# Multiply and GELU of two 1024 x 4096 arrays: all of x kept in SBUF, loads of 8192 down to 2048 columns, one store per 4096 columns

## The chip, the cores and the metric

The kernel runs on one core of one Trainium2 chip. The metric is device time of one execution in microseconds (us). Each profile is one execution; its span runs from the first instruction to the last, and the device time of the same execution is about 1.7 us longer. All runs quoted here were in the fast state, at clock 1.0.

## The reference

```python
def reference(x, y):            # two float32 arrays of 1024 x 4096
    z = x * y
    return (0.5 * z * (1 + np.tanh(np.sqrt(2 / np.pi) * (z + 0.044715 * z ** 3)))).astype(np.float32)
```

33.55 MB must be read and 16.78 MB written. Arithmetic is one multiply and one activation per element.

## The kernel before

Each array is seen as 128 partitions of 32768 columns. Seven tiles of 4096 columns and four of 1024 go through the same steps; x is overwritten by the product and by the result.

```python
def _process_tile(nc, sbuf, tile_f, x_r, y_r, out_r, c0, c1):
    ts_ = c1 - c0
    x_tile = sbuf.tile([128, tile_f], x_r.dtype)
    y_tile = sbuf.tile([128, tile_f], y_r.dtype)
    nc.sync.dma_start(out=x_tile[:, :ts_], in_=x_r[:, c0:c1])      # loads: SyncE queue
    nc.sync.dma_start(out=y_tile[:, :ts_], in_=y_r[:, c0:c1])
    nc.vector.tensor_mul(out=x_tile[:, :ts_], in0=x_tile[:, :ts_], in1=y_tile[:, :ts_])
    nc.scalar.activation(out=x_tile[:, :ts_], in_=x_tile[:, :ts_],
                         func=mybir.ActivationFunctionType.Gelu_apprx_tanh)
    nc.scalar.dma_start(out=out_r[:, c0:c1], in_=x_tile[:, :ts_])  # store: ScalarE queue
# ... (cut)
    big_tiles = [4096] * 7
    small_tiles = [1024] * 4
# ... (cut)
    big_sbuf = ctx.enter_context(tc.tile_pool(name="big", bufs=3))
    small_sbuf = ctx.enter_context(tc.tile_pool(name="small", bufs=8))
```

The stores are issued from the queue of the engine that does the activations.

## Time and profile before

| | before |
|---|---|
| device time, median of 4 runs | 123.83 us (123.77 to 123.91) |
| span of the profiled execution | 122.5 us |
| bytes moved, mean rate | 50.33 MB, 411 GB/s |
| VectorE / ScalarE busy | 35.8 / 30.7 us |

Read the DMA row of the page first: it is full in every slice but the first and the last, while both compute engines idle over two thirds of the time. A transfer-bound kernel like this one can lose time only where the transfer engines are empty or slow. The prediction below shows the lines.

### The profile page before, as it was taken

How to read it: one execution, taken by the hardware profiler on the slowest of the kernel's cores; microseconds unless marked ns; L12 is line 12 of the kernel's file. 1: busy time of each engine (PE TensorE's matmuls, PEld its weight loads, DVE VectorE, ACT ScalarE, POOL GpSimd, SP SyncE). 2: the span in 40 equal slices, each digit the busy share in tenths (PEclk: the TensorE clock that was granted, in tenths of full speed). 3: DMA queues.
4: the chain of work that ended last, by engine and by line, in shares of the span. 5: the costliest groups of instructions: out<-in, count | busy, mean ns of one | idle time of the engine just before them, and what ended most of it. 6: DMA issues, size and time to landing. Idle time of an engine off the chain costs nothing.

```text
span 122.5 us, 134 instructions
## 1 busy us (share of the span) xinstructions
DVE 35.8 (29%) x11; ACT 30.7 (25%) x12; POOL 0.2 (0%) x4
## 2 busy tenths in 40 slices
DVE  0000770590000580068000085019300039555000
ACT  4000029009100019001900004700650000884200
POOL 0000000000000000000000000000000000000000
DMA  4999999989999999999999999999999999999994
GB/s 112 428 433 428 439 439 433 369 337 439 439 433 428 433 428 428 428 433 428 428 433 439 439 433 433 428 428 433 433 428 428 428 417 407 411 413 455 397 423 164
DMA packets 4752, 50.33 MB, mean 411 GB/s; under 512 B 528, under 2 KB 528, under 8 KB 2064
## 3 DMA queue, kind: packets, MB, share of 16 engines
q1 hardware_dynamic: 3168, 33.56, 65.7%
q10 hardware_dynamic: 1584, 16.78, 32.2%
HBM read 33.55 MB, written 16.78 MB: 411 GB/s over the span
## 4 chain that ended last, share of the span: by engine, by line
DMA 76%; DVE 8%; ACT 7%; SPq 1%; issue 1%; DVEq 0%
DMA y_tile<-in_y_dram 30%; DMA out_dram<-x_tile 24%; DMA x_tile<-in_x_dram 22%; DVE x_tile L18 8%; ACT x_tile L20 7%; SPq L15 1%; SPq L16 0%; DVEq L18 0%
## 5 line engine op out<-in xcount | busy, mean ns | idle before, releaser
L18 DVE TENSOR_TENSOR x_tile<-x_tile,y_tile 128x4096 f32<-128x4096 f32 (+1 forms) x11 | 35.8, 3261 | 77.4 <-DMA y_tile<-in_y_dram 77.4
L20 ACT ACTIVATE x_tile<-x_tile 128x4096 f32<-128x4096 f32 (+1 forms) x11 | 29.4, 2684 | 82.8 <-DVE x_tile L18 82.4
L20 ACT ACT_TABLE_LOAD x1 | 1.3, 1283 | 0.7 <-PEq L87 0.7
L87 POOL MEMSET const-bfloat16-1.0<- 128x1 bf16 x1 | 0.1, 101 | 0.0
L87 POOL MEMSET const-uint8-127<- 128x1 uint8 x1 | 0.1, 101 | 0.0
L87 POOL MEMSET const-float32-0.0<- 128x1 f32 x1 | 0.1, 98 | 0.2 <-issue 0.2
L87 POOL MEMSET const-float32-1.0<- 128x1 f32 x1 | 0.1, 98 | 0.0
## 6 DMA issues: line engine op xcount, KB each, us to landing
x_tile<-in_x_dram SPq DMA_DIRECT2D x7, 2048.0 KB, 16.3
y_tile<-in_y_dram SPq DMA_DIRECT2D x7, 2048.0 KB, 20.7
out_dram<-x_tile ACTq DMA_DIRECT2D x7, 2048.0 KB, 13.8
x_tile<-in_x_dram SPq DMA_DIRECT2D x4, 512.0 KB, 21.2
y_tile<-in_y_dram SPq DMA_DIRECT2D x4, 512.0 KB, 20.5
out_dram<-x_tile ACTq DMA_DIRECT2D x4, 512.0 KB, 8.6
```

The source lines that it names most:

```text
L15: nc.sync.dma_start(out=x_tile[:, :ts_], in_=x_r[:, c0:c1])
L18: nc.vector.tensor_mul(out=x_tile[:, :ts_], in0=x_tile[:, :ts_], in1=y_tile[:, :ts_])
L20: nc.scalar.activation(out=x_tile[:, :ts_], in_=x_tile[:, :ts_], func=mybir.ActivationFunctionType.Gelu_apprx_tanh,)
L87: nc = _bacc.Bacc("TRN2", target_bir_lowering=False, num_devices=1)
```

## The change

The intent: no load should ever wait for a store to free its buffer. x gets a tile of its own for each load (128 KB per partition in all), y alternates between two buffers of 32 KB. Loads start at 8192 columns and shrink toward the end; compute and stores go in steps of 4096 columns (2048 for the last two loads).

```diff
+LOADS = [8192, 8192, 8192, 4096, 2048, 2048]
+STEP = 4096
 ...
-    big_sbuf = ctx.enter_context(tc.tile_pool(name="big", bufs=3))
-    small_sbuf = ctx.enter_context(tc.tile_pool(name="small", bufs=8))
 ... (the loop over tiles and _process_tile are removed)
+    x_pool = ctx.enter_context(tc.tile_pool(name="xs", bufs=1))
+    y_pool = ctx.enter_context(tc.tile_pool(name="ys", bufs=2))
+    a = 0
+    for i, w in enumerate(LOADS):
+        xt = x_pool.tile([P, w], F32, name=f"x{i}", tag=f"x{i}")
+        yt = y_pool.tile([P, max(LOADS)], F32, name=f"y{i}", tag="y")
+        nc.sync.dma_start(out=xt[:, :], in_=x_r[:, a : a + w])
+        nc.sync.dma_start(out=yt[:, :w], in_=y_r[:, a : a + w])
+        for c in range(0, w, STEP):
+            d = min(w, c + STEP)
+            nc.vector.tensor_mul(out=xt[:, c:d], in0=xt[:, c:d], in1=yt[:, c:d])
+            nc.scalar.activation(out=xt[:, c:d], in_=xt[:, c:d], func=GELU)
+            nc.scalar.dma_start(out=out_r[:, a + c : a + d], in_=xt[:, c:d])
+        a += w
```

Loads are called x0, y0 to x5, y5 below; the nine steps, their multiplies, activations and stores are numbered 0 to 8. Steps 0 to 6 have 4096 columns, steps 7 and 8 have 2048.

More of the change, by code (lines that the diff above doesn't have):

```diff
@@ L7 @@
 from concourse._compat import with_exitstack
-def _process_tile(nc, sbuf, tile_f, x_r, y_r, out_r, c0, c1):
-    ts_ = c1 - c0
-    x_tile = sbuf.tile([128, tile_f], x_r.dtype)
-    y_tile = sbuf.tile([128, tile_f], y_r.dtype)
-    nc.sync.dma_start(out=x_tile[:, :ts_], in_=x_r[:, c0:c1])
-    nc.sync.dma_start(out=y_tile[:, :ts_], in_=y_r[:, c0:c1])
-    nc.vector.tensor_mul(out=x_tile[:, :ts_], in0=x_tile[:, :ts_], in1=y_tile[:, :ts_])
-    nc.scalar.activation(
-        out=x_tile[:, :ts_],
-        in_=x_tile[:, :ts_],
-        func=mybir.ActivationFunctionType.Gelu_apprx_tanh,
-    )
-    nc.scalar.dma_start(out=out_r[:, c0:c1], in_=x_tile[:, :ts_])
+F32 = mybir.dt.float32
+GELU = mybir.ActivationFunctionType.Gelu_apprx_tanh
+LOADS = [8192, 8192, 8192, 4096, 2048, 2048]
+STEP = 4096
 @with_exitstack
@@ L42 @@
     out_r = out.flatten_outer_dims().rearrange("(p a) c -> p (a c)", p=P)
-    total_f = x_r.shape[1]
-    big_tiles = [4096] * 7
-    small_tiles = [1024] * 4
-    if sum(big_tiles) + sum(small_tiles) != total_f:
-        big_tiles = []
-        remaining = total_f
-        while remaining >= 4096 * 2:
-            big_tiles.append(4096)
-            remaining -= 4096
-        small_tiles = []
-        while remaining > 0:
-            ts_ = min(1024, remaining)
-            small_tiles.append(ts_)
-            remaining -= ts_
-    big_f = max(big_tiles) if big_tiles else 1024
-    small_f = max(small_tiles) if small_tiles else 1024
-    big_sbuf = ctx.enter_context(tc.tile_pool(name="big", bufs=3))
-    small_sbuf = ctx.enter_context(tc.tile_pool(name="small", bufs=8))
-    c0 = 0
-    for ts_ in big_tiles:
-        _process_tile(nc, big_sbuf, big_f, x_r, y_r, out_r, c0, c0 + ts_)
-        c0 += ts_
-    for ts_ in small_tiles:
-        _process_tile(nc, small_sbuf, small_f, x_r, y_r, out_r, c0, c0 + ts_)
-        c0 += ts_
+    assert sum(LOADS) == x_r.shape[1]
+    x_pool = ctx.enter_context(tc.tile_pool(name="xs", bufs=1))
[12 more added lines that the diff above has]
+        a += w
 _INS = ['x', 'y']
```

## The prediction

> **What bounds it now.** I read the page first (busy shares, GB/s by slice), then the chain that ended last, the groups by form, the windows, and last the trace's single DMA packet records.
>
> ```profile
> span 122.5 us, 134 instructions
> DVE 35.8 (29%) x11; ACT 30.7 (25%) x12; POOL 0.2 (0%) x4
> DMA  4999999989999999999999999999999999999994
> GB/s 112 428 433 428 439 439 433 369 337 439 439 433 428 433 428 428 428 433 428 428 433 439 439 433 433 428 428 433 433 428 428 428 417 407 411 413 455 397 423 164
> ...
> HBM read 33.55 MB, written 16.78 MB: 411 GB/s over the span
> ```
>
> The multiply engine and the activation engine are idle more than two thirds of the time; the transfers are busy in every slice but the first and last. 50.33 MB at the plateau of 431 GB/s is 116.8 us of the 122.5. So only three things can change the time: idle transfer engines at the start, in the middle, and at the end.
>
> ```profile
> 0.00:1.74 1.74, 0.00 (x0) 1.02 (x1) 0.20 (x4) 1.00 0.00 0
> ...
> 24.00:26.00 2.00, 2.00 (x1) 0.00 (x0) 0.00 (x0) 1.00 0.85 262
> 26.00:98.00 72.00, 19.01 (x5) 18.08 (x5) 0.00 (x0) 1.00 1.01 431
> 98.00:111.50 13.50, 8.01 (x4) 6.42 (x4) 0.00 (x0) 1.00 1.02 416
> 111.50:119.40 7.90, 1.22 (x1) 1.31 (x2) 0.00 (x0) 1.00 1.00 419
> ...
> 121.30:122.50 1.20, 0.00 (x0) 0.00 (x0) 0.00 (x0) 1.00 0.00 0
> ```
>
> (Columns: stretch, length, VectorE, ScalarE and GpSimd busy with counts, clock, DMA share, GB/s.) Lost now: 1.7 us before the first packet and about 1 us of slow first packets; (431-262) x 2 us = 0.34 MB, 0.8 us, when the first store begins; some 0.6 us to 1024-column transfers (416 and 419 over 21 us); 1.2 us of receipt and end. In the tail there is **no gap**: the last load's last packet ends at 111.4 us (packet records), and five stores of 4.19 MB in all are queued or about to be, which keep the engines busy to 121.3 us while the last tile is multiplied and activated:
>
> ```profile
> 111.95 1.22 DVE L18 TENSOR_TENSOR x_tile<-x_tile,y_tile 128x1024 f32<-128x1024 f32 x1 [1.29 <-DMA y_tile<-in_y_dram]
> 113.21 1.06 ACT L20 ACTIVATE x_tile<-x_tile 128x1024 f32<-128x1024 f32 x1 [1.46 <-DVE x_tile L18]
> 114.29 0.34 ACTq L26 DMA_DIRECT2D out_dram<-x_tile  x1
> ```
>
> **What the Trainium skill says.** "HBM Reference", Specifications, has a core streaming alone at about 425 GB/s; the trace agrees, 431. "SBUF — State Buffer", SBUF size, leaves about 208 KiB per partition; the change takes 128 KB of x and 64 KB of y, so it fits. "DMA: Bandwidth & Descriptors", Queues, rings and completion order, says that each engine takes a packet from one queue row, then from the next. The trace agrees, and shows what a packet is here: one partition's row of a transfer, 16384 B in 611 ns, or 4096 B in 159 ns. Where both queues hold 16384 B packets the load and store shares are near equal (in 2 us bins from 26.7 to 32.7 us the loads have 205, 152 and 225 GB/s, the stores 225, 279 and 206); where loads have 4096 B packets against stores of 16384 B, the bin at 98.7 to 100.7 us has 91 GB/s of loads and 339 of stores, 1 to 3.7. So **the queue with the longer rows gets more**. This decides the change.
>
> **The change part by part.**
> Removed: the waits of x loads for stores of the tile three before. In the DMA queue's waits these are the largest item:
>
> ```profile
> SPq L15 <- DMA out_dram<-x_tile: 78.7, 5, 32.8
> ```
>
> But loads were queued ahead, the engines never emptied, so it buys nothing by itself. Fewer and larger transfers (21 in place of 33, no 4096 B rows) give back about 0.5 us. The compute does not change: seven steps of 4096 columns and two of 2048.
>
> ```profile
> L18 DVE TENSOR_TENSOR x_tile<-x_tile,y_tile 128x4096 f32<-128x4096 f32 x7 | 31.0, 4425 | 73.5 <-DMA y_tile<-in_y_dram 73.5
> L20 ACT ACTIVATE x_tile<-x_tile 128x4096 f32<-128x4096 f32 x7 | 25.3, 3616 | 80.8 <-DVE x_tile L18 80.8
> L18 DVE TENSOR_TENSOR x_tile<-x_tile,y_tile 128x1024 f32<-128x1024 f32 x4 | 4.9, 1224 | 3.9 <-DMA y_tile<-in_y_dram 3.9
> L20 ACT ACTIVATE x_tile<-x_tile 128x1024 f32<-128x1024 f32 x4 | 4.2, 1052 | 2.0 <-DVE x_tile L18 1.6 <-ACT x_tile L20 0.4
> ```
>
> Interpolated between these, a 2048-column multiply is 1.22 + 1024 x (4.425-1.224)/3072 = 2.3 us, its activation 1.9.
>
> Added: a load wait on y's two buffers, a first store about 9 us later, and a last piece twice as large, whose load has short rows (8192 B). I work it with 0.43 MB/us, an effective start at 2.6 us, 0.5 us from last packet to multiply (12.61 to 13.09), 3.5 us from a store's issue to its first packet among loads (3.4 to 3.8 in the records), and shares in the ratio of row lengths.
> 1. x0 and y0, 8.39 MB: 22.1, landed 22.6. Multiplies end 27.0 and 31.5, stores 0 and 1 are issued at 30.7 and 35.1. y0's buffer is free at 31.5, so y2 is issued long before the queue needs it: that wait is hidden.
> 2. Until 34.2 the loads run alone: 13.6 MB. Then load rows of 32768 B meet store rows of 16384 B, 0.287 against 0.143 MB/us. With the 1 us lost at the first store, x1 and y1 (16.78 MB in all, 3.19 left) end at 34.2+1.0+3.19/0.287 = 46.3; stores 2 and 3 are issued at 54.9 and 59.4, y3 at 55.7.
> 3. x2 and y2, 8.39 MB at 0.287, take 29.2: 75.5. Stores 4 and 5 are issued at 84.1 and 88.6, y4 at 84.9.
> 4. x3 and y3 have rows equal to the stores', 0.215 each: 75.5+19.5 = 95.0. By then 9.97 MB is stored. y3's multiply ends 99.9 (y5 issued), store 6 is issued 103.6.
> 5. Now load rows are 8192 B: 0.143 against 0.287. Stores 4 and 5 are out at 104.1; loads alone until store 6 starts near 107; y4 ends 106.0, x5 111.2, store 6 at 114.4. Store 7 (issued 110.7) shares equally with y5: **y5 ends near 117.1**, store 7 at 118.2. Nothing else is queued.
> 6. y5 landed 117.6, multiply to 119.9, activation to 121.8, store 8 issued; the first packet some 2 us later (estimate: 1.0 us for the first load on idle engines, 2.5 for the 4096-column store issued at 108.13), 1.05 MB takes 2.4: 126.3, receipt and end 1.2: 127.5.
> So the engines stand empty some 5.6 us before the last store. Against 122.5 the span grows by about 5. Launch to span is 123.86-122.5 = 1.3 us, so 128.8 by this sum. Carried out packet by packet (the two queues taking turns, the packet durations above) the same arithmetic ends 0.5 to 2 us earlier; applied to the kernel before it ends 0.3 us from the real span.
>
> **Rivals.**
> (a) No gap: if stores lag more, or long rows are cut into packets of at most 8192 B, loads don't lose in the tail or earlier stores stay queued behind y5. Then 2.6+117.0+1.0+1.2 = 121.8 span, 123.1 us, same. For it: the queue was full throughout in the kernel before. Against: there the stores were held back by buffers and 4.19 MB remained after the last load; here each is sent at once and about 0.5 MB remains.
> (b) 32768 B rows travel as two packets of 16384 B. Then loads get half, not two thirds, while x1 to y2 load. Compute of load 2 comes later, so more store data is left over for the tail; packet by packet that gives 123 to 127 span, 124.3 to 128.3.
> (c) A y-buffer wait empties the engines in mid-run. Against: y2 is issued at 31.5 and needed at 60, y3 at 55.7 and needed at 85, y4 at 84.9 and needed at 102. Only y5, issued at 99.9, needed at 111, comes within 12 us. If a wait does bite there, 1 to 2 us more.
> (d) Long transfers run faster and larger steps save enough: at most the 0.6 us of small transfers, plus 0.8 us if the first store's dip vanished; 1.1%, not over 2%.
>
> **Range and chances.** The bound of 2% lies at 126.34 us, a span of 125.0. The main line (55%) gives 126.5 to 129.5; (b) (30%) is above the bound in under half its cases; (a) (15%) at 123 to 124.6. Together: middle 127.4, range 124.0 to 129.8; slower 0.62, same 0.35, faster 0.03.
>
> **What would show it.** Right: transfers empty for 3 to 7 us in the last slices, between the two last stores; the last multiply waiting for y, starting at 116 to 118 us; the last store issued at about 121; GB/s flat at about 430 from 5 to 115 us; loads having two thirds of the bytes from 35 to 75 us and a third after 95. Wrong: last load landed by 112, or DMA busy to the end. A median issue-to-landing of the stores much above 20 us would say that long rows starve the stores as I assume. A wait of the SP queue's last y load longer than to about 100 us would be rival (c).

## The result, and the profile after

The changed kernel takes **123.15 us** (median of 4 runs, 123.11 to 123.24) against 123.83. The ratio is 0.9945, 95% interval 0.9931 to 0.9959: half a per cent faster, where 127.4 and "slower" were expected. (Ratios here are the mean time of one kernel's fast runs over that of the other's fast runs of the same rounds, so not quite the ratio of the medians.)

The page of the changed kernel:

```profile
span 121.4 us, 104 instructions
DVE 35.3 (29%) x9; ACT 30.4 (25%) x10; POOL 0.2 (0%) x4
...
DMA  5899989999989989999999999999999999999994
GB/s 173 378 486 389 475 389 475 389 475 400 464 297 427 481 367 486 432 410 400 464 416 416 486 410 400 432 432 432 432 432 432 419 427 443 421 429 437 416 429 192
```

The DMA row is full up to the last slice: the gap of some 5.6 us that the prediction put before the last store isn't there. The GB/s row swings between 378 and 486 in slices 2 to 10 although nothing pauses; packets are 32768 B and 1.2 us long there, against slices of 3 us, so it depends on how many packets start in a slice. With the bytes of each packet spread evenly over its duration, the records give a flat 433 GB/s between 4 and 31 us. (The 297 in slice 12 is real: the slow stretch at the first store, taken up in the last experiments.)

The tail, in the timeline of the changed kernel (start, duration, engine; in brackets the idle time before and what ended it; ACTq is ScalarE's queue issuing a store):

```profile
83.35 0.34 ACTq L46 DMA_DIRECT2D out_dram<-x  x1
84.03 0.33 SPq L41 DMA_DIRECT2D y<-in_y_dram  x1
84.03 3.62 ACT L45 ACTIVATE x<-x 128x4096 f32<-128x4096 f32 x1 [0.72 <-DVE x L44]
...
99.22 3.62 ACT L45 ACTIVATE x<-x 128x4096 f32<-128x4096 f32 x1 [11.57 <-DVE x L44]
99.28 3.92 ACTq L46 DMA_DIRECT2D out_dram<-x  x2
...
111.24 2.29 DVE L44 TENSOR_TENSOR x<-x,y 128x2048 f32<-128x2048 f32 x1 [8.05 <-DMA y<-in_y_dram]
113.57 1.91 ACT L45 ACTIVATE x<-x 128x2048 f32<-128x2048 f32 x1 [8.40 <-DVE x L44]
113.63 2.22 ACTq L46 DMA_DIRECT2D out_dram<-x  x2
```

Activation 5 ends at 84.03 + 3.62 = 87.65 us, and its store is ready then. **No store is issued at 87.7.** The next entry of ScalarE is activation 6 at 99.22, and only after its start, at 99.28, come two stores: store 5, and store 6 when activation 6 is done. In the program as built, activation 6 stands ahead of store 5 on ScalarE's queue, so store 5 sat for 11.6 us behind an activation that was waiting for a multiply that was waiting for y3. (Store 5 also waits for a semaphore that store 3 had used, but that one was complete at 87.9 us by the trace's semaphore events, so it isn't what held the store.) The same stands in the tail: activation 8 is ahead of store 7, which was ready at 105.2 and went out at 113.63.

What this did to the transfers is read from the trace's records of single packets, which have start, duration, size and queue of each: store 4's last packet ends at 96.1 us, store 5's first starts at 102.7. In between the loads have the engines to themselves (428 GB/s of loads from 97 to 102 us, no stores), y4 and x5 are in by 102.9, and y5's last packet ends at 110.2. Stores 5, 6, 7 and 8 then keep the engines busy to 120.0. The windows of the changed kernel (stretch, length, busy time and count of VectorE, ScalarE and GpSimd, clock, DMA share, GB/s) show no empty stretch; a packet counts whole in the window in which it starts, so a share can pass 1:

```profile
85.00:96.10 11.10, 1.33 (x1) 2.65 (x1) 0.00 (x0) 1.00 1.01 430
96.10:102.70 6.60, 4.89 (x2) 3.48 (x1) 0.00 (x0) 1.00 1.00 425
102.70:110.20 7.50, 0.49 (x1) 2.05 (x2) 0.00 (x0) 1.00 1.05 449
110.20:115.10 4.90, 2.29 (x1) 1.53 (x1) 0.00 (x0) 1.00 0.95 408
115.10:120.00 4.90, 0.00 (x0) 0.38 (x1) 0.00 (x0) 1.00 0.95 398
```

The kernel before had shown the sign, in its own timeline: the seventh large activation and the first small one stand together, with their two stores after both.

```profile
104.49 4.56 ACT L20 ACTIVATE x_tile<-x_tile 128x4096 f32<-128x4096 f32 x2 [14.08 <-DVE x_tile L18]
...
108.13 1.28 ACTq L26 DMA_DIRECT2D out_dram<-x_tile  x2
```

There it cost nothing, as both activations' data was in. But it says plainly that the order on this queue isn't the order of the text.

### The profile page after: what moved, and what is told of

Same layout as the page of the kernel before. It is cut to its first block, busy times and chain, and to the rows that moved or that the text cites. A ratio compares the mean times of both kernels' runs of the same rounds, so it can differ in the third digit from the quotient of the medians.

```text
span 121.4 us, 104 instructions
## 1 busy us (share of the span) xinstructions
DVE 35.3 (29%) x9; ACT 30.4 (25%) x10; POOL 0.2 (0%) x4
## 4 chain that ended last, share of the span: by engine, by line
DMA 79%; DVE 13%; ACT 2%; SPq 1%; issue 0%; DVEq 0%
DMA y<-in_y_dram 79%; DVE x L44 13%; ACT x L45 2%; SPq L40 1%; SPq L41 0%; DVEq L44 0%
## 5 line engine op out<-in xcount | busy, mean ns | idle before, releaser
L44 DVE TENSOR_TENSOR x<-x,y 128x4096 f32<-128x4096 f32 (+1 forms) x9 | 35.3, 3949 | 78.2 <-DMA y<-in_y_dram 78.2
L45 ACT ACTIVATE x<-x 128x4096 f32<-128x4096 f32 (+1 forms) x9 | 29.1, 3237 | 72.1 <-DVE x L44 72.1
```

The source lines that it names most:

```text
L44: nc.vector.tensor_mul(out=xt[:, c:d], in0=xt[:, c:d], in1=yt[:, c:d])
L45: nc.scalar.activation(out=xt[:, c:d], in_=xt[:, c:d], func=GELU)
```

## The experiments

**Theory A.** The arithmetic of the prediction holds, except that store 5 was not issued when ready. Held back by 11.6 us, it let the last loads through and left enough to store behind them. **Theory B.** The order is irrelevant; enough bytes are stored late in any case. Later a third question came up, which store it is that must be held back. All variants gave correct results. The runs of the kernel before that went with them had medians of 123.86, 123.85 and 123.71 us.

### pin_all: every store as soon as its activation is done

```diff
-            nc.scalar.activation(out=xt[:, c:d], in_=xt[:, c:d], func=GELU)
+            g = nc.scalar.activation(out=xt[:, c:d], in_=xt[:, c:d], func=GELU)
+            tc.keep_in_program_order(g)     # stays behind the store written before it
```

> Every activation is kept behind the store before it, so each store is issued as soon as its activation is done, as the prediction assumed. Theory A (the program order on the ScalarE queue, with act 6 ahead of store 5, held store 5 back from 87.6 to 99.3 us and thereby saved the tail): store 5 issued at about 87, the last y load's last packet at 115 to 117 us in place of 110.2, a gap of 3.5 to 5.5 us in the transfers before the last store, span about 125.3, time about 127.0, 2.6% slower than the kernel before. Theory B (the order is irrelevant; the tail is full because enough bytes are stored late anyway): span 121.4, time 123.1, no gap.

Measured: **128.29 us** (128.02 to 128.55), ratio 1.0355 (1.0332 to 1.0378), span 126.7. The timeline of pin_all:

```profile
88.56 0.34 ACTq L47 DMA_DIRECT2D out_dram<-x  x1
...
117.57 2.29 DVE L44 TENSOR_TENSOR x<-x,y 128x2048 f32<-128x2048 f32 x1 [8.96 <-DMA y<-in_y_dram]
119.89 1.91 ACT L45 ACTIVATE x<-x 128x2048 f32<-128x2048 f32 x1 [9.35 <-DVE x L44]
121.83 0.34 ACTq L47 DMA_DIRECT2D out_dram<-x  x1
```

and its windows:

```profile
110.00:118.10 8.10, 0.53 (x1) 0.55 (x1) 0.00 (x0) 1.00 0.92 388
118.10:122.70 4.60, 1.76 (x1) 1.91 (x1) 0.00 (x0) 1.00 0.02 9
122.70:125.40 2.70, 0.00 (x0) 0.00 (x0) 0.00 (x0) 1.00 0.91 373
```

Store 5 goes out at 88.56, the last multiply starts 6.3 us later than in the changed kernel, and for 4.6 us the engines move nothing (no packet from 118.08 to 122.68 us; the 9 GB/s are packets that start at the window's end). These are the numbers of the prediction: its sum had store 5 at 88.6, the last multiply at 117.6, the last store at 121.8, and 128.8 us in the end. The expectation written for this run had the right gap but was 1.3 us low in the total (127.0). Theory B falls: the same loads, buffers and stores in another order on one queue cost 5.1 us.

### pin_store5, pin_store7 and pin_but_last: which store has to be late

pin_store5 pins the activations up to number 6, pin_store7 only the last one.

```diff
+            if a + c <= 24576:            # pin_store5   (pin_store7: if a + c == 30720)
+                tc.keep_in_program_order(g)
```

> Only stores 0 to 6 before the activation of columns 28672 are pinned; the last two activations still stand ahead of store 7. Theory A says store 5 is the one that matters: span about 125.2, the last y load's end at about 115. Rival A2 (the held-back store 7 is what keeps the tail full): span 121.4.

> Only store 7 is freed from waiting behind the last activation: issued at about 105.2 in place of 113.6 us. Theory A: it queues behind store 6, which holds the queue until 115, so nothing moves: span 121.3 to 121.6, time about 123.1. Rival A2: store 7 in the queue early takes packets from the last y load and a gap opens: span 123 or more.

pin_store7: 123.20 us (123.10 to 123.26), ratio 0.9943, span 121.4. Store 7 went out at 105.23 in place of 113.63, and nothing else moved, as expected: its first packet came at 114.8, behind store 6.

pin_store5 was a miss for theory A as it was written: 123.27 us (123.08 to 123.65), ratio 0.9945, not 127. Its timeline says why:

```profile
99.74 3.62 ACT L45 ACTIVATE x<-x 128x4096 f32<-128x4096 f32 x1 [11.21 <-DVE x L44]
...
108.59 1.91 ACT L45 ACTIVATE x<-x 128x2048 f32<-128x2048 f32 x1 [5.23 <-DVE x L44]
108.65 2.22 ACTq L48 DMA_DIRECT2D out_dram<-x  x2
```

Store 5 was issued at 88.56, but now the program as built had activation 7 ahead of store 6. Store 6, ready at 103.4, waited until 108.65; its first packet came at 110.2, and y5 was in at 110.7. The hold had only changed stores. (Seven activations are pinned here and the time is that of the changed kernel, so pinning by itself costs nothing.) So I restated the theory: one 2 MB store, 5 or 6, must wait until the last loads are nearly in; the last 1 MB before the end isn't enough. pin_but_last is the run that pin_store5 was meant to be: stores 0 to 6 each at once, only store 7 behind the last activation.

```diff
+            if a + c < 30720:
+                g = nc.scalar.activation(out=xt[:, c:d], in_=xt[:, c:d], func=GELU)
+                tc.keep_in_program_order(g)
+            else:
+                with tc.issue_after(g.ins):   # behind activation 7, free to pass store 7
+                    nc.scalar.activation(out=xt[:, c:d], in_=xt[:, c:d], func=GELU)
```

> Stores 0 to 6 each at once (both 5 and 6 ahead of the next activation), only store 7 still behind the last activation: what pin_store5 was meant to be, where the scheduler put activation 7 ahead of store 6 instead. Theory A2 (restated: one 2 MB store must be kept back until the last loads are in; store 5 or 6 does it, the 1 MB store 7 alone doesn't): the last y load ends at 114.5 to 116.5 us, a gap of 3.5 to 5 us, now ahead of store 7, span 125.5 to 126.7, time 127.3 to 128.4. Rival (pin_store5 was fast because store 5 at once does no harm, and pin_all slow because of store 7): span 121.4 to 121.9.

Measured: 127.33 us (127.00 to 127.47), ratio 1.0285 (1.0269 to 1.0302), span 125.6. Stores 5 and 6 went out at 88.11 and 103.29, as soon as they were ready, and store 7 only at 118.23; y5's last packet came at 115.5, and there is a window of pin_but_last with nothing in it, ahead of store 7:

```profile
116.00:119.00 3.00, 2.14 (x1) 0.83 (x1) 0.00 (x0) 1.00 0.00 0
```

The gap is 3.6 us by the packet records (115.5 to 119.1). The restated theory stands.

### pin_halves: every store at once, but with short rows

If store 5 does harm because its 16384 B rows take two thirds of the engines from loads with 8192 B rows, then cutting the rows should undo the harm without delaying any store.

```diff
+            n = 2 if 16384 <= a + c < 28672 else 1      # stores 4, 5 and 6 in two halves
+            for e in range(c, d, (d - c) // n):
+                f = e + (d - c) // n
+                nc.scalar.dma_start(out=out_r[:, a + e : a + f], in_=xt[:, e:f])
```

(on top of pin_all)

> As pin_all, every store at once, but stores 4, 5 and 6 go out as two halves of 2048 columns, rows of 8192 B in place of 16384 B. Theory A with the share by row length: beside the short load rows the loads now get half, not a third; the last y load ends at about 111.5 and no gap opens: span about 121.5, time about 123.2. If only the moment of the store's issue matters and not its rows: span as pin_all, about 125.

Measured: 123.41 us (123.31 to 123.62), ratio 0.9963, span 121.5. y5's last packet ends at 111.9 (116.9 in pin_all). Loads and stores share 214 to 213 GB/s from 94 to 100 us, where pin_all has 134 to 297 between 97 and 101. Its windows have no gap:

```profile
93.70:110.00 16.30, 6.00 (x2) 5.53 (x2) 0.00 (x0) 1.00 1.01 428
110.00:117.00 7.00, 2.29 (x1) 1.91 (x1) 0.00 (x0) 1.00 1.01 427
```

One qualification: the second half of store 5 was issued at 92.9 in place of about 88.3, since in the built program it waits for a semaphore that, by the moment, y3's load still used (that load's last packet ended at 92.2). It began to move at 103.5 only, behind the halves before it, so this wait didn't decide anything. **The row length by itself closes the gap.**

### tail_1024, before_tail_2048 and short_loads: where the half per cent came from

```diff
-LOADS = [8192, 8192, 8192, 4096, 2048, 2048]
+LOADS = [8192, 8192, 8192, 4096, 1024, 1024, 1024, 1024]      # tail_1024
```

> The changed kernel with the last 4096 columns loaded and stored as four pieces of 1024 in place of two of 2048: rows of 4096 B again. If the gain of 0.68 us comes from the rows in the tail: back to about 123.5 to 123.7 us. If it comes from the buffers or the long loads: stays at 123.15.

Measured: 127.11 us (126.69 to 127.42), ratio 1.0263. A clear miss, and not an answer to its question. With two y buffers, four small y loads can't be queued ahead: the second was issued at 99.4, the third at 100.6 and the last at 108.25, once the multiply of the load two before it had freed the buffer. By then stores 5 and 6 were in the queue with rows four times as long as the loads', the last y load ended at 118.5, and the engines were empty from 119.4 to 121.3. It is the same trap from another side: short load rows beside long store rows.

```diff
-    small_tiles = [1024] * 4                     # before_tail_2048: the kernel before,
+    small_tiles = [2048] * 2                     # two last tiles of 2048, small pool bufs=2
```

> The kernel before with two last tiles of 2048 columns in place of four of 1024, nothing else. If the gain comes from the rows in the tail: 123.3 to 123.5 us, half or more of the gain. If it comes from the long loads or from x in its own tiles: stays at 123.83. Risk: with rows of 8192 B and the store of 4096 columns, the last tile is later by some 1 us and the queue may run short.

Measured: median 123.59 us, but 123.50 to 124.49 over six runs; ratio 0.9993, interval 0.9969 to 1.0017. Inconclusive.

```diff
-LOADS = [8192, 8192, 8192, 4096, 2048, 2048]    ... name="ys", bufs=2
+LOADS = [4096] * 7 + [2048] * 2                 ... name="ys", bufs=4      # short_loads
```

> The changed kernel with loads of 4096 columns (seven, then two of 2048) and four y buffers of 16 KB in place of loads of 8192 and two of 32 KB; x stays in own tiles. If the gain of 0.7 us comes from the tail's longer rows: about 123.2 to 123.4 us. If the long loads give it: back to about 123.7. Stores are issued at once in its program order except the one of the first 2048-column tile; loads and stores have equal rows until the tail, so the last y load should end near 111 and no gap open.

Measured: 123.55 us against 123.71 of the kernel before in the same rounds, ratio 0.9985 (0.9972 to 0.9998). y5's counterpart ended at 110.6 and there was no gap, as expected. So x in its own tiles and the longer rows in the tail together give, by these ratios, under a third of the gain (0.15% of 0.55%), and the long loads, it seems, most of it; this run also has four y buffers in place of two, which wasn't tried alone. One account goes some way with both. The median packet durations are

| row of a packet | 4096 B | 8192 B | 16384 B | 32768 B |
|---|---|---|---|---|
| duration | 159 ns | 309 ns | 611 ns | 1213 ns |

From 16384 to 32768 B a packet takes 602 ns more; at that rate per byte each of the four lengths leaves 8 to 9 ns over (611 - 602, 309 - 301, 159 - 150.5). Each packet thus costs some 8.5 ns on top of its bytes. The kernel before has 4224 data packets, 264 per engine; the changed one 2688, 168 per engine; short_loads 3456, 216 per engine. By this estimate the changed kernel saves 96 x 8.5 ns = 0.8 us (measured: 0.68) and short_loads 48 x 8.5 ns = 0.4 us (measured: 0.16). The direction and the order fit; executions of one kernel differ by 0.2 us and more, so the split isn't settled closer than that.

### y0_act and early_store: the slow stretch when stores begin

Both kernels lose about 0.6 to 1.0 us where the first store starts (bytes missing against 432 GB/s, packets spread evenly: 0.6 us in the changed kernel, 1.0 in the kernel before). If that could be avoided, a version faster than both would follow.

```diff
-        nc.sync.dma_start(out=yt[:, :w], in_=y_r[:, a : a + w])                              # y0_act
+        (nc.scalar if i == 0 else nc.sync).dma_start(out=yt[:, :w], in_=y_r[:, a : a + w])
 ...
+    et = e_pool.tile([P, 64], F32, name="e0", tag="e0")                                       # early_store
+    nc.vector.memset(et[:, :], 0.0)
+    nc.scalar.dma_start(out=out_r[:, 0:64], in_=et[:, :])     # overwritten by store 0
```

> The changed kernel with its first y load issued from the ScalarE queue in place of the SyncE queue. Both kernels lose 0.8 to 0.9 us when the first store starts (262 GB/s for 2 us before, 360 GB/s for 5 us after). If that is the first use of the ScalarE transfer queue: the dip at 31 to 36 us is gone and the time falls to about 122.4. If it belongs to the first write to HBM: the dip stays and so does the time, 123.15.

> The changed kernel plus a store of 64 columns of zeros at the very start, overwritten later. The slow stretch at the first store stayed when the ScalarE queue had carried a load before (y0_act: 380 GB/s over 31 to 36 us). If it is paid once, at the first write to HBM: the stretch at 31 to 36 us recovers to about 430, and the time falls by up to 0.7 us, unless the early store itself slows the first loads by as much. If it belongs to every start of stores beside loads: no change, 123.15.

y0_act: 123.18 us (123.11 to 123.37), ratio 0.9950. The stretch stayed. The same window, first of the changed kernel:

```profile
31.00:36.00 5.00, 0.44 (x1) 3.62 (x1) 0.00 (x0) 1.00 0.96 360
```

then of y0_act:

```profile
31.00:36.00 5.00, 0.50 (x1) 3.62 (x1) 0.00 (x0) 1.00 0.96 380
```

So it isn't the first use of ScalarE's transfer queue: spread evenly, both kernels lose 0.6 us between 30 and 45 us. early_store: 124.01 us, but 123.19 to 124.52 over six runs, ratio 1.0003 (0.9970 to 1.0037), so nothing was gained. Its profiled execution was one of the longer ones, at 122.7 us, but the packet records of its start still show the stretch: 376, 346, 320 and 379 GB/s in the four microseconds from 34 to 38, about 0.8 us lost. In this one trace, then, a small write at the start did not take the stretch away. The cause of the stretch stays open, and no variant beat the changed kernel clearly; pin_store7 and y0_act equal it.

## Why the prediction was wrong, point by point

- **What bounds the kernel: right.** The transfer engines bound it before and after; compute changed by half a microsecond at most, as said.
- **Step 1: right but for the first store.** First multiply at 22.68 (22.6 predicted); y2 was issued at 31.47 and waited for nothing that mattered. Store 0, ready at 30.76, went out at 31.48, just after activation 1 had started: the error of step 3 already, worth 0.7 us here.
- **Step 2 and 3: right but for one term.** y1 ended at 45.2 (46.3), y2 at 74.3 (75.5), with the loads at 286 and the stores at 144 GB/s from 36 to 45 us, the predicted two to one. Store 4 was issued at 83.35 (84.1). **The term that failed is in step 3: "Stores 4 and 5 are issued at 84.1 and 88.6".** Store 5 was issued at 99.28. I took the stores to be issued in the order of the text, and never asked where they stand on ScalarE's queue. Why the framework built that order wasn't looked into.
- **Step 4: right**, since it rests on store 4 only up to its end: equal shares (216 to 216 from 78 to 84 us), y3 ended at 93.7 (95.0).
- **Steps 5 and 6: wrong in the changed kernel, right in pin_all.** With store 5 absent, x4 to x5 had the engines alone, y5 ended at 110.2 in place of 117.1, and stores 5 to 8 filled the rest; the sign of being wrong that was named in advance, "last load landed by 112", came. With store 5 at 88.56, the steps came true within about a microsecond and the total within 0.5 us (128.8 predicted, 128.29 measured). That total owes something to luck: for the profiled execution, the predicted span of 127.5 was 0.8 us too long (126.7), and the 1.3 us from span to device time were 0.5 too short (1.8). Between the two orders of one queue lie 5.1 us.
- **Rival (a), no gap: this is what happened**, for half of the first reason that I gave, a store that lags. I had argued against it with "here each is sent at once", the same unchecked assumption. Its 123.1 us meets the measured 123.15, but it named no cause for the lag and was given 15%. Rival (b) is out: rows of 32768 B travel as one packet of 1213 ns. Rival (c) is out for the changed kernel, y5 was issued at 99.22 and needed at 102.6; with smaller pieces it did bite (tail_1024).
- **The gain: too small.** "About 0.5 us" from fewer and larger transfers; by packet counts an estimated 0.8, and 0.68 was measured. Rival (d) is half right: larger transfers do save, but the prediction put its 0.6 us down to the 1024-column transfers (its own figures, 416 and 419 against 431 GB/s, make 0.7), and the long loads seem to give the larger part. And the 1.3 us from span to device time came from the slow specimen of the profile; in all runs it is about 1.7.
- **The chances.** The alternatives were about row lengths, buffers and speeds. None varied the order on ScalarE's queue, though two lines of the trace before show that order. The result lay in rival (a)'s own 123 to 124.6, and the range, which began at 124.0, left that part out.

## What to carry to other kernels

Before a sum rests on when a transfer is issued, read the order of that engine's queue in the trace or in the built program: a transfer issued from a compute engine's queue goes out when its turn comes, not when its data is ready. In a transfer-bound kernel the last loads decide the end, so keep about as much store work waiting behind them as the last multiply, activation and issue take, and don't let long-row stores run beside short-row loads there. A good result may depend on an order that nobody chose; test it by pinning the order, as pin_all does, since the same text in its written order was 4% slower than what was built.

## What the Trainium skill lacked or had wrong

- "DMA: Bandwidth & Descriptors", Queues, rings and completion order, says that an engine takes turns between queue rows at packet granularity. The runs agree, but a packet in the trace was one row of one partition, up to 32768 B, not 9 to 17 descriptors; in the changed kernel from 50 to 58 us, where each record is followed to the one that starts as it ends, load rows and store rows alternate one for one. The page doesn't draw the consequence: shares follow row lengths, 286 to 144 GB/s for 32768 B beside 16384 B, 134 to 297 for 8192 B beside 16384 B, 214 to 213 for equal rows.
- The same page, Anatomy of one DMA, says (of another path for issuing transfers, but in general words) that a semaphore wait happens on the issuing sequencer before dispatch. It doesn't say what that means for stores issued from a compute engine: store 5 was ready at 87.65 us and went out at 99.28, behind an activation that waited for something else.
- The same page, Why small descriptors are slow, gives a fixed overhead of about 3 cycles per packet. Here each packet cost about 8.5 ns beyond its bytes at all four lengths (159, 309, 611 and 1213 ns), worth an estimated 0.8 us of this kernel at rows far above the sizes that the page calls small. No run shows whether it is the same overhead.
- No page has the slow stretch at the first store beside running loads: 360 GB/s over 5 us in the changed kernel, 262 over 2 us in the kernel before, still there when ScalarE's queue had carried a load first (380 over the same 5 us) or a small store (320 to 379 from 34 to 38 us). Its cause is open.
